# Three moves of order and engine in a four-part encoder trunk: units side by side, a multiply on GpSimd, rows split in two parts

## The chip, the cores and the metric

The kernel runs on one core of a Trainium2 chip. The core has TensorE (matrix products, called PE in the profile; its weight loads are PEld), VectorE (DVE), ScalarE (ACT), GpSimd (POOL) and SyncE (SP, which here issues transfers). The metric is the device time of one execution in microseconds. Before the change three runs took 2383.26, 2383.97 and 2384.84 us; their median is 2383.97 us.

## The reference

An encoder trunk of two layers over 512 positions of width 1024, in float32:

```python
def swiglu(x, w_gu, w_down):
    g, u = jnp.split(x @ w_gu, 2, axis=-1)
    return (jax.nn.silu(g) * u) @ w_down
...
for i in range(DEPTH):
    h = h + 0.5 * swiglu(rmsnorm(h, ffn1_norm[i]), ffn1_w_gu[i], ffn1_w_down[i])
    hn = rmsnorm(h, mix_norm[i])
    # layer 0: ssd_mixer(hn, ...), a state space scan in both directions
    # layer 1: neighbourhood_attention(hn, ...)
    h = h + 0.5 * swiglu(rmsnorm(h, ffn2_norm[i]), ffn2_w_gu[i], ffn2_w_down[i])
    gate = jax.nn.sigmoid(rmsnorm(h, ple_norm[i]) @ ple_w_gate[i])
    h = h + gate * rmsnorm(p[i] @ ple_w_proj[i], ple_post_norm[i])
```

`rmsnorm(x, g)` is x times the reciprocal root of its mean square times a gain g. Inside the SSD mixer the projection of hn has 65 blocks of 128 columns; behind the scan stand another rmsnorm (over 2048 columns) and the output product.

## The kernel before, in words

**Layout.** Activations lie transposed: 128 features on the partitions, 512 positions along the free axis. The residual `h` is eight such tiles. A matrix product in float32 is made of three products in the reduced type fp32r: each operand is cut into a high part and a low part, and `gemm` (L176) issues, for each of eight (or seven) k blocks, high weight times high data (L181), high weight times low data (L184) and low weight times high data (L185). A **unit** is one 128 x 1024 block of weights, so 24 matmuls of 128x512.

**Weights.** `plan` (L121) gives all units in the order of use. `load_unit` (L153) has SP fetch one into `wr` (4 buffers), `split_unit` (L161) makes the high part `wh` on ACT (L166) and the low part `wl` on DVE (L168), with 3 buffers each, and `unit` (L171) keeps three units made ahead of TensorE. So the buffers of a unit are free for the third one behind it when its last matmul has read them.

**Data.** `split(dst, src, gain)` (L187) cuts data in the same way. Without a gain it is a copy on ACT (L189) and a subtraction on DVE (L190); with a gain it is an ACT activation with a scale (L192) and a DVE scalar_tensor_tensor (L193). `Norm.prep` (L256) does this for each residual tile as soon as it is final, with the gain of the next norm, and has the square of the tile summed (L213 on ACT, L217 on GpSimd, or on DVE for the last tile). The norm's factor per position, R, comes later from that sum (`factor`, `rsqrt`, L219: a matmul with ones at L221, then eleven DVE operations, L199 to L205) and is multiplied into the products, not into the data.

**Feed-forward.** `ffn` (L279) runs 22 pairs of units (gate and up) in three chunks, with the chunk's down units behind each. For the first pair the gate unit's eight k blocks run first, then the up unit's eight, then R is made. `activate` (L311) multiplies by R on DVE (L313, L317), takes SiLU on ACT and multiplies the two on GpSimd (L318). There are four feed-forwards; the very first one has an order of its own (`first`). The third follows the gated embedding of layer 0 (`ple`, L377), whose last tile takes a DVE multiply, a tanh on ACT, and two more DVE operations in two halves (L388 to L391), and then `prep`.

**SSD.** `ssd` (L419) begins with unit `ptd` (step sizes) and the first unit of group 0, and makes R between (L435). Units 1 and 2 of group 0 still use the data without R (`norm.pairs`), and their convolution multiplies R in (`conv`, L506, L509). From unit 3 on, the data are `xn`, with R and gain multiplied in: the loop at L450 to L454 makes each of the eight tiles on DVE (L452), then splits it without a gain (L189, L190). `steps` (L456) works out step sizes and decays with many small DVE operations, and writes rows to DRAM (`crow`, `vrow`), from which ACT's L558 reads later. `project` (L523) runs eight units a group; `conv` is one ACT activation (L513), four DVE operations (L517), a tanh (L520) and a DVE product (L521). `scan` (L563) is a generator whose steps run between the next group's units: transposes on TensorE (L577), copied by ACT (L581), multiplied on GpSimd (L585), and so on.

**SSD output.** The output product over 2048 columns is done in two halves of eight row tiles each. The rows 0 to 7 lie in DRAM, are fetched by `early_rows` (L729) at the sixth of group 7's eight units, and are split with the norm's gain by `pairs_of` (L740: L192, L193). Before the change all eight are split at the eighth of these units (i == 7, L773), ahead of the last group's first scan step, whose transposes need ACT too. `out_half` (L751) then runs the first half's units between the last group's scan steps.

**Attention.** `keys` (L817) runs units 0 to 3, then 4 to 7; after unit 0 it makes R. Products lie in five PSUM banks (`mm_bank`); `px_bank` has three more.

**Order.** The program is written in the order of the code, but a planner that builds it sets the order on each engine: it walks through the program with planned durations, and gives an engine that comes free the ready instruction that stands first in the code. At run time each engine follows that order strictly, and waits where an input is late. So a matmul whose input the planner holds to be late can be passed by later ones; one whose input is late only at run time can't.

Of the kernel before, what the change touches and what calls it, by code (L numbers as in the profile page):

```python
# [47 lines left out]
def trunk(ctx, tc, A, out):  # L48
# [55 lines left out]
    def col(i):  # L104
        return cst[:, i:i + 1]
# [70 lines left out]
    def gemm(pt, w, pairs, first=True, last=True, off=0, cols=slice(0, T), behind=False):  # L176
        hi, lo = w
        n = len(pairs)
        for k, xp in enumerate(pairs):
            sl = slice((off + k) * P, (off + k + 1) * P)  # L180
            m = te.matmul(out=pt, lhsT=hi[:, sl], rhs=xp[:, 0, cols], start=first and k == 0, stop=False)  # L181
            if behind and k == 0:
                tc.keep_in_program_order(m)
            te.matmul(out=pt, lhsT=hi[:, sl], rhs=xp[:, 1, cols], start=False, stop=False)  # L184
            te.matmul(out=pt, lhsT=lo[:, sl], rhs=xp[:, 0, cols], start=False, stop=last and k == n - 1)  # L185

    def split(dst, src, gain):  # L187
        if gain is None:
            cast = s.copy(out=dst[:, 0, :], in_=src)  # L189
            v.tensor_sub(out=dst[:, 1, :], in0=src, in1=dst[:, 0, :])  # L190
        else:
            cast = s.activation(out=dst[:, 0, :], in_=src, func=AF.Copy, scale=gain)  # L192
            v.scalar_tensor_tensor(out=dst[:, 1, :], in0=src, scalar=gain, in1=dst[:, 0, :],  # L193
                                   op0=ALU.mult, op1=ALU.subtract)
        return cast
# [83 lines left out]
    def ffn(norm, nxt, between=lambda: None, first=None):  # L279
        R = [None]  # L280
        mids = {}

        held = []

        def gate_up(f):
            pg = mm_bank()
            if not (first and R[0] is None and f == 2):
                pu = mm_bank()
            if first and f < 2:
                held.append((f, pg, pu))  # L290
                if f == 1:
                    first([p for x in held for p in x[1:]], norm.pairs)
                    norm.begin()
                return
            gemm(pg, unit(), norm.pairs)
            if first and R[0] is None:
                pu, w = px_bank(), unit()
                gemm(pu, w, norm.pairs[:4], last=False)
                R[0] = norm.end()
                while held:  # L300
                    activate(*held.pop(0))
                gemm(pu, w, norm.pairs[4:], first=False, off=4)
            else:
                gemm(pu, unit(), norm.pairs)
            if R[0] is None:
                R[0] = norm.factor()
            held.append((f, pg, pu))
            while held:
                activate(*held.pop(0))

        def activate(f, pg, pu):  # L311
            gm = t2()
            v.tensor_mul(out=gm, in0=pg, in1=R[0])  # L313
            sg = sc()
            s.activation(out=sg, in_=gm, func=AF.Silu)
            um = t2()
            v.tensor_mul(out=um, in0=pu, in1=R[0])  # L317
            g.tensor_mul(out=um, in0=um, in1=sg)  # L318
            m = md(F32R)
            split(m, um, None)  # L320
            mids[f] = m

        def down(c, finish=None):
            a, b = CHUNKS[c]
            for d in range(KD):
                pt = mm_bank()
                gemm(pt, unit(), [mids[f] for f in range(a, b)])
                v.scalar_tensor_tensor(out=h[d], in0=pt, scalar=0.5, in1=h[d], op0=ALU.mult, op1=ALU.add)  # L328
                if c == len(CHUNKS) - 1:
                    nxt(d)  # L330
                if d == 2 and finish is not None:
                    finish()

        for c in range(len(CHUNKS)):
            for f in range(*CHUNKS[c]):
                gate_up(f)
            if c:
                down(c - 1)
        made = between()
        if made is None:  # L340
            down(len(CHUNKS) - 1)
            return
        down(len(CHUNKS) - 1, made[1])
        return made[0]
# [74 lines left out]
    def ssd(norm, nxt):  # L419
# [29 lines left out]
        xn = []  # L449
        for k in range(KD):  # L450
            t = t2()
            v.scalar_tensor_tensor(out=t, in0=hk[k], scalar=col(norm.gain + k), in1=R, op0=ALU.mult, op1=ALU.mult)  # L452
            xn.append(md(F32R))
            split(xn[k], t, None)  # L454

        def steps():  # L456

# [307 lines left out]
        for gi in range(NG):  # L765
            beside = project(gi + 1) if gi + 1 < NG else out_half()
            sn = scan(gi, *cur, e0)
            if gi == NG - 1:
                next(sn)
            for i, r in enumerate(beside):  # L770
                cur = r
                if i == 7 and gi == NG - 2:
                    prs = pairs_of(range(8))  # L773
                next(sn, None)
                if i == 5 and gi == NG - 2:
                    early_rows()
                if i == 6 and gi + 1 < NG:
                    e0 = expo(gi + 1, 0)
# [31 lines left out]
    def attention(norm, nxt):  # L810
# [6 lines left out]
        def keys(js):  # L817

            nonlocal R
            kst = px_bank()  # L820
            raw = []
            for j in js:
                pt = mm_bank()
                gemm(pt, unit(), norm.pairs)
                if R is None:
                    R = norm.factor()
                if j % 2 == 0:
                    kt = md()
                kj = kt[:, j % 2, :]
                v.tensor_mul(out=kj, in0=pt, in1=R)  # L830
                q = t2()
                s.activation(out=q, in_=kj, func=AF.Square)
                o = M_SEL + 16 * j + 2 * js[0]
                te.matmul(out=kst[:8], lhsT=msk[:, o:o + 8], rhs=q, start=j == js[0], stop=j == js[-1])
                raw.append(kj)
            m, rk, ra = sc(), sc(), sc()
            v.tensor_scalar(out=m[:8], in0=kst[:8], scalar1=EPS, scalar2=None, op0=ALU.add)
            newton_rsqrt(m[:8], rk[:8], ra[:8])
            rkd = dp.tile([8, T], F32, name=nm("rkd"))
            sy.dma_start(out=rkd, in_=rk[:8])  # L840
            for i in range(4):
                rb = sc()
                for a in range(2):
                    r_ = slice(a * 64, (a + 1) * 64)
                    sy.dma_start(out=rb[r_], in_=rkd[2 * i + a:2 * i + a + 1, :].to_broadcast([64, T]))
                v.scalar_tensor_tensor(out=rb, in0=raw[i], scalar=gqk, in1=rb, op0=ALU.mult, op1=ALU.mult)
                kn = md(F32R)
                split(kn, rb, None)
                kz.append(kn)
# [328 lines left out]
```

## Time and profile before

| | |
|---|---|
| median of three runs | 2383.97 us |
| the profiled execution's own time | 2384.19 us |
| its span on the core | 2382.4 us |
| TensorE busy | 2368.6 us |
| VectorE busy | 1414.6 us |
| ScalarE busy | 957.3 us |
| GpSimd busy | 443.3 us |
| mean granted TensorE clock | 0.999 |

The page of the profile gives busy time by engine, and groups of instructions by line. A row of a group reads: line, engine, operation, out<-in by the program's names, count, then busy time and mean duration, then the idle time of the engine just before these instructions and what ended it. A row of the timeline reads: start, duration (both in us from the span's start), engine, line, operation, count of merged instructions, and in brackets the idle time before and its releaser. Matmuls overlap: one of 128x512 is shown with some 0.39 us, but the next starts some 0.23 us after it, so what is lost on TensorE is read from the distance of two starts. A row of the waits reads: engine and line, whom it waited for, us in total, times, the longest.

### The profile page before, as it was taken

The page shows a single profiled execution, that of the slowest core. Times are in us where ns is not written, and L with a number is a line of the kernel's source. Part 1 is how long each engine was busy: PE and PEld are TensorE (multiplying, and loading weights), DVE is VectorE, ACT ScalarE, POOL GpSimd, SP SyncE. Part 2 cuts the span into 40 slices and gives each one's busy share as a digit, 9 for nine tenths or more (in the row PEclk, how much of TensorE's full clock was granted, in tenths as well). Part 3 has the DMA queues.
Part 4 walks back from the last instruction along what each step waited for, and adds up shares of the span by engine and source line. Part 5 has one row for each costly group of instructions (what it writes and reads, how often), then busy time and mean ns, then how long its engine had stood idle before and what let it go on. Part 6 is the DMA issues. An engine that isn't in the chain of part 4 may idle for free.

```text
span 2382.4 us, 29262 instructions
## 1 busy us (share of the span) xinstructions
PE 2368.6 (99%) x11464; PEld 1953.0 (82%) x11464; DVE 1414.6 (59%) x1893; ACT 957.3 (40%) x1560; POOL 443.3 (19%) x373
## 2 busy tenths in 40 slices
PE   9999999999999999999999999999999999999999
PEld 8888888888888888888888788888877888888887
DVE  6453447877777858554446755444568855544456
ACT  5222324655555653322224433222337753322242
POOL 1110100444555541110103111000100011100120
PEclk9999999999999999999999999999999999999999
DMA  5333233544444452333333233333433332233332
GB/s 180 98 96 99 90 119 104 169 134 142 142 141 139 157 166 89 98 97 97 95 104 102 80 97 97 98 97 93 138 111 136 98 100 92 95 99 97 106 89 80
DMA packets 89707, 265.58 MB, mean 111 GB/s; under 512 B 10960, under 2 KB 11856, under 8 KB 89568
## 3 DMA queue, kind: packets, MB, share of 16 engines
q1 hardware_dynamic: 89280, 263.56, 35.0%
q8 instruction: 90, 1.47, 0.3%
q14 instruction: 49, 0.40, 0.1%
q10 hardware_dynamic: 288, 0.14, 0.0%
HBM read 253.40 MB, written 10.26 MB: 111 GB/s over the span
## 4 chain that ended last, share of the span: by engine, by line
PE 93%; DVE 4%; ACT 2%; issue 1%; DMA 1%; SPq 0%; POOL 0%; DVEq 0%; ACTq 0%; POOLq 0%
PE ps L181 28%; PE ps L184 28%; PE ps L185 28%; PE ps L657 1%; DVE wl L168 1%; PE ps L635 1%; PE ps L678 1%; PE ps L591 1%; PE ps L577 1%; PE ps L958 1%; PE ps L948 0%; DVE md L193 0%; DVE md L190 0%; PE ps L905 0%; PE ps L939 0%
## 5 line engine op out<-in xcount | busy, mean ns | idle before, releaser
L181 PE MATMUL ps<-md,wh 128*128 128x512 f32 (+1 forms) x3152 | 1236.7, 392 | 3.1 <-ACT md L192 3.1
L185 PE MATMUL ps<-md,wl 128*128 128x512 f32 (+1 forms) x3152 | 1228.5, 390 | 0.7 <-DVE wl L168 0.7
L184 PE MATMUL ps<-md,wh 128*128 128x512 f32 (+1 forms) x3152 | 1227.9, 390 | 0.3 <-DVE md L193 0.3
L166 ACT CAST wh<-wr 128x1024 fp32r<-128x1024 f32 (+1 forms) x401 | 414.7, 1034 | 1019.6 <-PE ps L184 638.7
L181 PEld LDWEIGHTS ps<-md,wh 128*128 128x128 f32 x3152 | 592.3, 188 | 128.2 <-issue 4.2
L184 PEld LDWEIGHTS ps<-md,wh 128*128 128x128 f32 x3152 | 592.3, 188 | 125.2 <-issue 4.9
L185 PEld LDWEIGHTS ps<-md,wl 128*128 128x128 f32 x3152 | 592.2, 188 | 124.9 <-DVE wl L168 1.3
L168 DVE TENSOR_TENSOR wl<-wr,wh 128x1024 fp32r<-128x1024 f32 (+1 forms) x401 | 576.8, 1438 | 157.5 <-ACT wh L166 131.8
L318 POOL TENSOR_TENSOR t<-t,sc 128x512 f32<-128x512 f32 x88 | 122.7, 1396 | 1033.0 <-ACT wh L166 635.4
L217 POOL TENSOR_TENSOR sq<-sq,sq 128x512 f32<-128x512 f32 x71 | 104.9, 1478 | 602.6 <-ACT sq L213 600.2
L317 DVE TENSOR_TENSOR t<-ps,rt 128x512 f32<-128x512 f32 x88 | 60.7, 690 | 258.6 <-PE ps L185 258.6
L328 DVE SCALAR_TENSOR_TENSOR hs<-ps,hs 128x512 f32<-128x512 f32 x96 | 66.3, 691 | 233.0 <-PE ps L185 233.0
L313 DVE TENSOR_TENSOR t<-ps,rt 128x512 f32<-128x512 f32 x88 | 60.8, 690 | 127.9 <-PE ps L185 125.6
L517 DVE SCALAR_TENSOR_TENSOR t<-ps,ccw,t 128x510 f32<-128x510 f32 (+1 forms) x180 | 134.0, 745 | 3.1 <-ACT t L513 0.3
L570 POOL TENSOR_TENSOR sc<-sc,sc 128x512 f32<-128x512 f32 x64 | 98.1, 1552 | 66.3 <-ACT sc L560 66.2
L189 ACT CAST md<-t 128x512 fp32r<-128x512 f32 x96 | 59.4, 623 | 121.3 <-POOL t L318 119.3
L558 ACT ACTIVATE sc<-hs,md 128x128 f32<-128x128 f32 x256 | 82.4, 396 | 2.9 <-DMA hs<-crow 2.9
L190 DVE TENSOR_TENSOR md<-t,md 128x512 fp32r<-128x512 f32 x96 | 67.9, 711 | 18.9 <-ACT md L189 18.4
L192 ACT ACTIVATE md<-hs,cst 128x512 fp32r<-128x512 f32 x64 | 46.0, 723 | 50.2 <-DVE hs L798 19.8
L520 ACT ACTIVATE t<-t 128x512 f32<-128x512 f32 x48 | 30.2, 630 | 78.6 <-DVE t L517 78.0
L585 POOL TENSOR_TENSOR md<-md,md 128x256 f32<-128x256 f32 x64 | 45.9, 751 | 84.1 <-ACT md L581 84.1
L193 DVE SCALAR_TENSOR_TENSOR md<-hs,cst,md 128x512 fp32r<-128x512 f32 x64 | 50.6, 794 | 13.7 <-ACT md L192 13.7
(169 smaller groups left out, 1366.7 us busy)
## 6 DMA issues: line engine op xcount, KB each, us to landing
wr<-in_w_gu_dram SPq DMA_DIRECT2D x172, 512.0 KB, 3.5
wr<-in_w_in_dram SPq DMA_DIRECT2D x65, 512.0 KB, 3.6
wr<-in_w_dn_dram SPq DMA_DIRECT2D x64, 448.0 KB, 3.3
wr<-in_w_dn_dram SPq DMA_DIRECT2D x32, 512.0 KB, 3.5
hs<-crow SPq DMA_DIRECT2D x64, 256.0 KB, 3.8
wr<-in_w_qkv_dram SPq DMA_DIRECT2D x24, 512.0 KB, 3.5
hs<-vrow SPq DMA_DIRECT2D x64, 128.0 KB, 4.0
wr<-in_w_out_dram SPq DMA_DIRECT2D x16, 512.0 KB, 4.2
```

The lines of the kernel that those rows point to most:

```text
L166: splits.append(s.copy(out=hi[:, :n], in_=raw[:, :n]))
L168: v.tensor_sub(out=lo[:, :n], in0=raw[:, :n], in1=hi[:, :n])
L181: m = te.matmul(out=pt, lhsT=hi[:, sl], rhs=xp[:, 0, cols], start=first and k == 0, stop=False)
L184: te.matmul(out=pt, lhsT=hi[:, sl], rhs=xp[:, 1, cols], start=False, stop=False)
L185: te.matmul(out=pt, lhsT=lo[:, sl], rhs=xp[:, 0, cols], start=False, stop=last and k == n - 1)
L190: v.tensor_sub(out=dst[:, 1, :], in0=src, in1=dst[:, 0, :])
L217: (v if fast else g).tensor_add(out=self.acc, in0=self.acc, in1=q)
L318: g.tensor_mul(out=um, in0=um, in1=sg)
L328: v.scalar_tensor_tensor(out=h[d], in0=pt, scalar=0.5, in1=h[d], op0=ALU.mult, op1=ALU.add)
L517: v.scalar_tensor_tensor(out=a[:, lo:hi], in0=src[:, lo + o:hi + o], scalar=w(j), in1=a[:, lo:hi], op0=ALU.mult, op1=ALU.add)
L558: s.activation(out=e[:, cs(c)], in_=cb[:, cs(c)], func=AF.Relu, scale=-1.0, bias=cum[:, dr, c, hd:hd + 1])
L570: g.tensor_mul(out=es[j], in0=es[j], in1=cbm[j % 2])
```

## The change

Three edits. A new helper, `side_by_side`, takes two units at once: seven k blocks of the first, seven of the second, then the eighth of each. The feed-forwards other than the first use it for their first pair, and `keys` for its first two units; in `keys` R is made after both. In `ssd` the multiply that makes `xn` is done on GpSimd without the gain, and the gain goes into the split. The row tiles 4 to 7 of the SSD output are split after the first scan step of the last group.

```diff
+    def side_by_side(pts, pairs, behind=False):
+
+        ws = [unit() for _ in pts]
+        k = len(pairs) - 1
+        for pt, w in zip(pts, ws):
+            gemm(pt, w, pairs[:k], last=False, behind=behind)
+            behind = False
+        for pt, w in zip(pts, ws):
+            gemm(pt, w, pairs[k:], first=False, off=k)
...
-            gemm(pg, unit(), norm.pairs)
+            if R[0] is None and not first:
+                side_by_side((pg, pu), norm.pairs)
+            else:
+                gemm(pg, unit(), norm.pairs)
...
-            else:
+            elif R[0] is not None:
                 gemm(pu, unit(), norm.pairs)
...
-            v.scalar_tensor_tensor(out=t, in0=hk[k], scalar=col(norm.gain + k), in1=R, op0=ALU.mult, op1=ALU.mult)
+            g.tensor_mul(out=t, in0=hk[k], in1=R)
             xn.append(md(F32R))
-            split(xn[k], t, None)
+            split(xn[k], t, col(norm.gain + k))
...
             if gi == NG - 1:
                 next(sn)
+                prs += pairs_of(range(4, 8))
...
                 if i == 7 and gi == NG - 2:
-                    prs = pairs_of(range(8))
+                    prs = pairs_of(range(4))
...
-                pt = mm_bank()
-                gemm(pt, unit(), norm.pairs)
-                if R is None:
+                if j == 0:
+                    pts = [mm_bank(), mm_bank()]
+                    side_by_side(pts, norm.pairs)
                     R = norm.factor()
+                if j < 2:
+                    pt = pts[j]
+                else:
+                    pt = mm_bank()
+                    gemm(pt, unit(), norm.pairs)
```

## The prediction

> **What bounds the kernel now.** First the page and its busy times, then who TensorE waits for over the whole span.
>
> ```profile
> span 2382.4 us, 29262 instructions
> ...
> PE 2368.6 (99%) x11464; PEld 1953.0 (82%) x11464; DVE 1414.6 (59%) x1893; ACT 957.3 (40%) x1560; POOL 443.3 (19%) x373
> ```
>
> ```profile
> PE ps L181 <- ACT md L192: 3.4, 2, 3.1
> PE ps L577 <- ACT md L581: 1.3, 1, 1.3
> PE ps L577 <- DVE md L521: 1.1, 1, 1.1
> ...
> PE ps L185 <- DVE wl L168: 0.7, 1, 0.7
> ```
>
> TensorE is the bound: 2368.6 of 2382.4 us. The change takes no matmul away, so it can only win back waits, and there are few: the four rows come to 6.5 us. Four places matter, and each is looked at in the timeline.
>
> *Place 1, the third feed-forward, behind the gated embedding.* TensorE, then VectorE, then ScalarE, then the clock:
>
> ```profile
> 1348.61 0.39 PE L184 MATMUL ps<-md,wh 128*128 128x512 f32 x1
> 1348.84 0.39 PE L185 MATMUL ps<-md,wl 128*128 128x512 f32 x1
> 1352.32 0.73 PE L181 MATMUL ps<-md,wh 128*128 128x512 f32 x2 [3.09 <-ACT md L192]
> 1353.11 0.50 PE L184 MATMUL ps<-md,wh 128*128 128x512 f32 x1
> ```
>
> ```profile
> 1348.62 1.55 DVE L168 TENSOR_TENSOR wl<-wr,wh 128x1024 fp32r<-128x1024 f32 x1
> 1350.10 0.75 DVE L390 SCALAR_TENSOR_TENSOR t<-t,md 128x256 f32<-128x256 f32 x2
> 1350.77 0.75 DVE L391 TENSOR_TENSOR hs<-hs,t 128x256 f32<-128x256 f32 x2
> 1352.30 0.75 DVE L193 SCALAR_TENSOR_TENSOR md<-hs,cst,md 128x512 fp32r<-128x512 f32 x1 [0.79 <-ACT md L192]
> ```
>
> ```profile
> 1351.55 0.72 ACT L192 ACTIVATE md<-hs,cst 128x512 fp32r<-128x512 f32 x1 [2.34 <-DVE hs L391]
> ```
>
> ```profile
> 1353.00:1356.50 3.50, 3.45 (x10) 2.68 (x10) 1.88 (x3) 1.04 (x1) 0.00 (x0) 0.59 0.03 11
> 1356.50:1360.00 3.50, 3.50 (x15) 2.85 (x15) 0.00 (x0) 0.00 (x0) 0.00 (x0) 0.93 0.44 150
> ```
>
> Matmuls start 0.23 us apart (1348.61, 1348.84). At 1349.07 TensorE has done seven of the gate unit's eight k blocks; the eighth tile's high part is ready only at 1352.27, since VectorE made a weight remainder (L168) ahead of the embedding's last operations. Then the granted clock (seventh column of the windows) falls to 0.59 and 0.93. Lost: 1352.32 - 1348.84 - 0.23 = 3.25; two matmuls and a small wait up to 1353.11, 0.79 - 0.46 = 0.33; clock, 0.41 x 3.5 + 0.07 x 3.5 = 1.7. Together some **5.2 us**.
>
> *Place 2, the second feed-forward, behind the SSD:*
>
> ```profile
> 931.34 0.39 PE L181 MATMUL ps<-md,wh 128*128 128x512 f32 x1
> 932.01 0.50 PE L184 MATMUL ps<-md,wh 128*128 128x512 f32 x1 [0.28 <-DVE md L193]
> ```
>
> 0.67 - 0.23, and 0.1 on the slower matmul behind it: **0.55 us**.
>
> *Place 3, the SSD's start.* Windows by engine (PE, PEld, DVE, ACT, POOL), then VectorE's groups from 380 to 392:
>
> ```profile
> 380.00:397.70 17.70, 17.70 (x81) 14.38 (x81) 17.53 (x27) 10.12 (x17) 0.00 (x0) 1.00 0.18 56
> 397.70:416.00 18.30, 17.65 (x78) 14.27 (x77) 17.57 (x30) 6.79 (x9) 1.61 (x2) 1.00 0.28 91
> ```
>
> ```profile
> L452 DVE SCALAR_TENSOR_TENSOR t<-hs,cst,rt 128x512 f32<-128x512 f32 x8 | 5.5, 735 | 0.0
> L190 DVE TENSOR_TENSOR md<-t,md 128x512 fp32r<-128x512 f32 x8 | 5.0, 676 | 0.0
> ```
>
> VectorE has no gap for 36 us (35.1 busy), GpSimd does nothing in the first half. TensorE loses a little at 410:
>
> ```profile
> 409.20 0.39 PE L181 MATMUL ps<-md,wh 128*128 128x512 f32 x1
> 409.43 0.39 PE L184 MATMUL ps<-md,wh 128*128 128x512 f32 x1
> 409.65 0.39 PE L181 MATMUL ps<-md,wh 128*128 128x512 f32 x1
> 409.88 0.39 PE L184 MATMUL ps<-md,wh 128*128 128x512 f32 x1
> 410.92 0.50 PE L185 MATMUL ps<-md,wl 128*128 128x512 f32 x1 [0.65 <-DVE wl L168]
> ```
>
> ```profile
> 409.65 1.22 DVE L168 TENSOR_TENSOR wl<-wr,wh 128x1024 fp32r<-128x1024 f32 x1
> ```
>
> 1.04 - 0.23 = 0.8 us for a weight remainder. The order is telling: two pairs L181, L184 before the first L185, so the planner knew the remainder to be late and passed one L185, but not by enough. Later there is the wait of 1.1 us for L521 (second fence):
>
> ```profile
> 431.99 0.99 ACT L558 ACTIVATE sc<-hs,md 128x128 f32<-128x128 f32 x3 [2.85 <-DMA hs<-crow]
> 432.88 0.61 ACT L520 ACTIVATE t<-t 128x512 f32<-128x512 f32 x1
> ```
>
> ScalarE stood 2.85 us for the decay rows from DRAM with L520, which L521 needs, queued behind.
>
> *Place 4, the SSD output's rows,* on ScalarE:
>
> ```profile
> 822.51 0.58 ACT L539 ACTIVATE t<-ps 128x512 f32<-128x512 f32 x1
> 822.99 1.94 ACT L192 ACTIVATE md<-t,cst 128x512 fp32r<-128x512 f32 x3
> 824.83 1.05 ACT L581 COPY md<-ps 128x512 f32<-128x512 f32 x2
> ```
>
> Three row splits stand ahead of the copies for which TensorE waits 1.3 us.
>
> **The change part by part.**
>
> *Feed-forwards.* Nothing is added to any engine but order. Seven k blocks of the up unit, 21 x 0.23 = 4.8 us, go between 1349.07 and the gate unit's eighth block, so this block starts at 1353.9. Its parts are ready at 1352.27 and 1353.05 (1352.30 + 0.75): 1.6 and 0.8 us of cover. The wait goes, and with it the low clock: **-5.2**. If the cover were gone, TensorE would wait for the excess alone. Next in line would be weights: the gate unit's buffers come free 4.8 us later, at 1354.5; the next cast (some 1.0) and remainder (up to 1.55, L168 above) end by 1357.2, and that unit is wanted at 1353.9 + 6 x 0.23 + 24 x 0.23 = 1360.8. SP's fetch of one weight unit moves up with the second `unit` call; it waits for a raw buffer as before. Place 2: **-0.55**. The fourth feed-forward has no wait of TensorE at its start: 0.
>
> *Keys.* No row of TensorE's waits lies there: 0 to win. R comes one unit (5.5 us) later; first use now:
>
> ```profile
> 1726.47 1.89 DVE L830 TENSOR_TENSOR md<-ps,rt 128x512 f32<-128x512 f32 x3
> ```
>
> From 1726.5 it goes to 1732; three products already wait there, and unit 3 ends only behind that. Five banks cover it; if they ran out, TensorE would wait for the excess. Cost 0.
>
> *Rows.* Two of the three splits of 1.94 us (rows 4 and 5) go behind L581, which then starts 1.3 us earlier: the wait of 1.3 shrinks to some 0.2, **-1.1**. Their place is taken by the first blocks of the output product (rows 0 to 3: 12 x 0.23 = 2.8 us) and the scan's own matmuls, so rows 4 and 5 have time. No transfer moves: the rows' fetches stay where they are. Bounds: -1.3, and +0.5 if row 4 came late.
>
> *Multiply on GpSimd.* Eight L452 leave VectorE (5.5 us), its eight remainders turn from 0.68 into 0.75 (L193 at 1352.30; +0.6), ScalarE's casts cost 0.1 more each. GpSimd gets eight multiplies of two SBUF tensors. The trace has no such multiply here; the nearest group is of the same size, with min/median/max:
>
> ```profile
> L570 POOL TENSOR_TENSOR sc<-sc,sc x64: 1272/1297/2290, 447.1 to 855.6; 128x512 f32<-128x512 f32 x64
> ```
>
> So 1.3 us alone and 2.3 at worst, that is 10.4 to 18.3 us for eight, from 380.2. How they stand to VectorE is seen at 838.6, where a pair of them meets a weight remainder, which takes 1.22 us by itself (409.65):
>
> ```profile
> 838.58 2.40 DVE L168 TENSOR_TENSOR wl<-wr,wh 128x1024 fp32r<-128x1024 f32 x1 [5.04 <-ACT wh L166]
> ```
>
> ```profile
> 838.59 3.54 POOL L570 TENSOR_TENSOR sc<-sc,sc 128x512 f32<-128x512 f32 x2
> ```
>
> VectorE needs 2.40, its own 1.22 and nearly one multiply; the pair needs 3.54, its own 2.6 and nearly one remainder. They take turns and don't overlap. By the Trainium skill (SBUF — State Buffer, section "SBUF: two separate sides") the two engines share a port pair under an exclusive lock, which a VectorE operation with two SBUF inputs contends for against GpSimd, and the loser blocks for the whole instruction. By that rule the multiplies are not free beside the splits; the trace agrees, with 2.40 against 1.22.
>
> Now VectorE step by step. 380.2 to 380.9 L446, then L509 (from PSUM, 0.7). From 382.8 each remainder of `xn` (two SBUF inputs, 0.75) waits for a multiply of 1.3: first remainder 383.5, a weight remainder 386.0, then 388.0, 390.05, 392.1, 394.15, 396.2; GpSimd is through, and the last two end at 396.95 and 397.7. TensorE reads the eighth at some 397.8 (unit 3 starts at 392.8, 0.68 a block): just in time. But VectorE's other work is late. By 397.7 it had done 17.5 - 5.5 - 5.0 = 7.0 us of it; now it has done 0.7 + 0.7 + 1.2 = 2.6. It is **4.4 us behind** in a stretch where it has no gap, so the remainder of 409.65 would come 4.4 us later. The planner can cover that by passing L185s: 16 of a unit's 24 matmuls need no remainder, four ran, so 12 x 0.23 = 2.7 more. Left: **+1.7** (bounds: -1.9, if nothing is lost to turns and both waits, 0.8 and 1.1, go; +4.4, if nothing is passed). I take 1.7, as the rows show both the turns and the passing. The wait for L521 I leave at 1.1: decays and convolution move together.
>
> Sum: -5.2 - 0.55 - 1.1 + 1.7 = -5.15. The profiled execution took 2384.19 us (span 2382.4 and 1.8 around it), 0.2 above the median of 2383.97: 2384.19 - 5.15 = **2379.0 us**.
>
> **The rivals.**
>
> *A: GpSimd frees VectorE.* If the turns are cheaper than at 838.6, the 5.5 us taken off VectorE end both waits: -6.85 - 1.9, **2375.4**. For it: GpSimd idle, VectorE without a gap. Against it: 2.40 for 1.22.
>
> *B: the 4.4 us are not covered.* The planner holds VectorE faster than it is (it passed one L185 where four were wanted), so it might pass too few: -6.85 + 4.4, **2381.7**.
>
> *C: the side-by-side order doesn't meet the wait,* because the second unit's split, now earlier in the code, pushes the embedding's last operations on VectorE back by the time won. Then place 1 stays as it is: -0.55 - 1.1 + 1.7 + about 0.6 for the later weights, **2384.8**. Against it: that split has to wait for the gate unit's buffers, free only at 1354.5.
>
> *D, slower than before: VectorE's lag reaches TensorE twice.* The place is the SSD's start: 4.4 us at the weight remainder and 4.4 again at L577 near 433, as the decay rows come late and ScalarE's order holds L520 behind them. Each idle stretch is then over 3.09 us, after which the clock fell at place 1 (1.7 us each, so 3.4): 12.2 - 6.85 = +5.35, **2389.5**. It decides from 6.85 us lost at the SSD's start. For it: 2.85 us of ScalarE's wait for `crow`. Against it: TensorE's first delay gives the second chain the same time. The Trainium skill (TensorE: Matmul & The Clock Gate, section "What's actually happening") has the clock halve after an idle window of about 3.4 us; here 3.09 us of idling were enough, so D's condition goes by the row.
>
> **How the numbers follow.** Forecast 0.40, A 0.28, B 0.20, C 0.05, D 0.07. A measurement of this kernel tells about 0.2% from no change: 4.8 us, so faster is below 2379.2 and slower above 2388.7. The forecast lies on the edge; half of it counts as faster. Faster: 0.28 + 0.20 = 0.48. Slower: D, 0.07. Same: 0.45. Range: A to B with about 1.5 us for the rows and the small terms above, and the same below cut to 0.6, since A already takes every wait away: **2374.8 to 2383.2**, leaving out C and D. The forecast's own range is 2377 to 2381.
>
> **What would show it.** Place 1: no idle TensorE before the eighth block and a granted clock of 1.00 there; a wait left would speak for C. Place 3: GpSimd's eight multiplies at over 1.3 us mean and VectorE's remainders at over 0.75, L185s passed in the units after unit 3, and a wait of TensorE on `wl`; no such wait speaks for A, one of 3 us and more for B, two for D. Place 4: L581 right behind one L192. Keys: no wait. Wrong altogether would be a planner that puts the work of the SSD's start in another order on VectorE than the step by step above.

## The result, and the profile after

The changed kernel takes 2387.41 us (median of 22 runs, 2386.24 to 2389.18) against 2384.28 us of the kernel before (22 runs on the same chips): ratio 1.0014, 95% interval 1.0008 to 1.0021, so 3.1 us slower. The prediction, 2379.0 us with a range of 2374.8 to 2383.2, is wrong, and in the other direction.

Lines of the changed kernel are shifted: L192, L193 are now L202, L203 (split with gain); L452 is L465, on GpSimd; L477 and L481 (last operation of the decays, and the matmul that reads it) are L490 and L494; L509, L517, L520, L521 (convolution) are L522, L530, L533, L534; L577, L581 are L590, L594; L687, L688 are L700, L701. L166 to L185 keep their numbers.

The page, and whom TensorE waits for:

```profile
span 2387.3 us, 29267 instructions
...
PE 2372.0 (99%) x11464; PEld 1957.0 (82%) x11464; DVE 1411.8 (59%) x1885; ACT 957.9 (40%) x1560; POOL 456.9 (19%) x381
```

```profile
PE ps L184 <- DVE md L203: 2.8, 3, 2.0
PE ps L181 <- ACT wh L166: 1.8, 1, 1.8
PE ps L494 <- DVE md L490: 1.4, 1, 1.4
PE ps L590 <- ACT md L594: 1.3, 1, 1.3
...
PE ps L185 <- DVE wl L168: 1.1, 2, 0.7
```

VectorE is busy only 2.8 us less, although eight operations of 0.7 us left it, and TensorE is busy 3.4 us longer for the same 11464 matmuls, mostly for a lower clock. The old wait of 3.1 us for L192 is gone; four new ones stand in its place (two in the row of L203, one each for L166 and L490), while that for the copies (L594) is as long as before. Compared matmul by matmul (times of the kernel before), the profiled execution falls 5.2 us behind in the SSD's start (by 452 us) and another 6.0 us at the SSD output's rows (by 836 us). It wins back 0.6 us in the second feed-forward (932 us) and 5.3 us in the third (by 1361 us); the span is 4.9 us longer. This execution took 2389.18 us, the longest of the 22, and its mean granted clock of 0.997 is the lowest of them. One at 1.000 took 2386.47 us, so the loss does not hang on a lower clock alone.

**Place 1, the third feed-forward.** TensorE is 10.5 us late here, so the stretch that began at 1349.07 begins at 1359.6. The eighth tile's high part on ScalarE, its first matmul on TensorE, then windows of TensorE, VectorE and so on, with the granted clock in the seventh column:

```profile
1362.11 0.72 ACT L202 ACTIVATE md<-hs,cst 128x512 fp32r<-128x512 f32 x1 [2.35 <-DVE hs L404]
```

```profile
1364.37 0.39 PE L181 MATMUL ps<-md,wh 128*128 128x512 f32 x1
```

```profile
1359.60:1363.00 3.40, 3.40 (x16) 2.82 (x15) 2.61 (x6) 1.05 (x3) 0.05 (x1) 1.00 0.32 83
1363.00:1366.50 3.50, 3.50 (x16) 2.63 (x14) 1.56 (x3) 1.78 (x3) 0.00 (x0) 1.00 0.17 69
```

The high part is ready at 1362.83, 1.5 us before TensorE comes to it. TensorE has no gap, and the clock stays at 1.00 where it was 0.59 before.

**Place 3, the SSD's start.** First the eight multiplies on GpSimd (min/median/max in ns), then VectorE's eight remainders:

```profile
L465 POOL TENSOR_TENSOR t<-hs,rt x8: 1289/1735/1742, 380.3 to 391.3; 128x512 f32<-128x512 f32 x8
```

```profile
L203 DVE SCALAR_TENSOR_TENSOR md<-t,cst,md 128x512 fp32r<-128x512 f32 x8 | 10.5, 1310 | 3.1 <-ACT md L202 3.1
```

A multiply takes 1.29 us alone and 1.74 in turn with a remainder; a remainder 1.31 instead of 0.75. With 3.1 us of waiting between them, VectorE spends 13.6 us on the eight, where the sixteen operations before took 10.5. ScalarE and TensorE at the end of this stretch:

```profile
393.05 0.72 ACT L202 ACTIVATE md<-t,cst 128x512 fp32r<-128x512 f32 x1 [0.97 <-POOL t L465]
393.67 1.98 ACT L166 CAST wh<-wr 128x1024 fp32r<-128x1024 f32 x2
```

```profile
394.75 0.50 PE L181 MATMUL ps<-md,wh 128*128 128x512 f32 x1 [1.83 <-ACT wh L166]
395.09 0.56 PE L184 MATMUL ps<-md,wh 128*128 128x512 f32 x1
396.34 0.79 PE L185 MATMUL ps<-md,wl 128*128 128x512 f32 x1 [0.70 <-DVE wl L168]
396.93 0.63 PE L181 MATMUL ps<-md,wh 128*128 128x512 f32 x1
397.36 0.63 PE L184 MATMUL ps<-md,wh 128*128 128x512 f32 x1
```

The weight casts of units 3 and 4 stand on ScalarE behind all eight L202, six of which wait 0.97 us each for GpSimd. In the kernel before they stood between the copies of the tiles:

```profile
381.51 1.04 ACT L166 CAST wh<-wr 128x1024 fp32r<-128x1024 f32 x1
387.12 1.05 ACT L166 CAST wh<-wr 128x1024 fp32r<-128x1024 f32 x1
```

So TensorE waits 1.83 us for a cast, then 0.70 for the remainder behind it, and from 396.93 two matmuls start 0.43 us apart instead of 0.23: the clock is halved. The third piece comes later, at the matmuls that read the decays, on VectorE and TensorE:

```profile
419.44 0.41 DVE L490 SCALAR_TENSOR_TENSOR md<-md,ea 128x256 f32<-128x256 f32 x1
```

```profile
420.00 1.13 PE L494 MATMUL ps<-md,msk 128*128 128x128 f32 x8 [1.44 <-DVE md L490]
```

VectorE finishes the decays at 419.85, 3.5 us later than L477 in the kernel before (416.39).

**Place 4, the rows.** ScalarE, VectorE, GpSimd, TensorE, and the windows' clock:

```profile
828.78 1.03 ACT L166 CAST wh<-wr 128x1024 fp32r<-128x1024 f32 x1
829.72 1.07 ACT L594 COPY md<-ps 128x512 f32<-128x512 f32 x2
```

```profile
830.41 1.21 DVE L168 TENSOR_TENSOR wl<-wr,wh 128x1024 fp32r<-128x1024 f32 x1
835.22 1.09 DVE L701 TENSOR_TENSOR sc<-sc,md 128x512 f32<-128x512 f32 x1 [3.59 <-POOL sc L700]
...
836.83 1.07 DVE L203 SCALAR_TENSOR_TENSOR md<-t,cst,md 128x512 fp32r<-128x512 f32 x1
```

```profile
833.60 0.61 POOL L598 TENSOR_TENSOR md<-md,md 128x256 f32<-128x256 f32 x1
834.17 1.01 POOL L700 TENSOR_TENSOR sc<-sc,hs 128x384 f32<-128x384 f32 x1
```

```profile
837.95 0.50 PE L184 MATMUL ps<-md,wh 128*128 128x512 f32 x1 [1.95 <-DVE md L203]
```

```profile
838.89:845.70 6.81, 6.19 (x16) 4.80 (x16) 1.83 (x2) 6.01 (x16) 6.81 (x9) 0.50 0.51 148
```

The copies that TensorE waits for hardly started earlier: they come 1.97 us after the first of the transposes, 2.20 us before the change, since a weight cast (L166) took the place on ScalarE that the splits left. And row 4's remainder, moved back, now stands on VectorE behind L701 (the gate's product of an output tile of the scan), which waits 3.59 us for GpSimd's L700 (the sum of that tile), itself queued among GpSimd's multiplies L598. Row 5's split waits on ScalarE as well, behind the square of that tile. TensorE waits 1.95 and 0.62 us, and runs 6.8 us at half clock from 838.89 on. In the kernel before, VectorE stood at the same spot, with no row behind it:

```profile
831.25 1.08 DVE L688 TENSOR_TENSOR sc<-sc,md 128x512 f32<-128x512 f32 x1 [3.15 <-POOL sc L687]
```

### The profile page after: what moved, and what is told of

It is laid out like the page before. It is cut to its first block, busy times and chain, and to the rows that moved or that the text cites. A ratio compares the mean times of both kernels' runs of the same rounds, so it can differ in the third digit from the quotient of the medians.

```text
span 2387.3 us, 29267 instructions
## 1 busy us (share of the span) xinstructions
PE 2372.0 (99%) x11464; PEld 1957.0 (82%) x11464; DVE 1411.8 (59%) x1885; ACT 957.9 (40%) x1560; POOL 456.9 (19%) x381
## 4 chain that ended last, share of the span: by engine, by line
PE 94%; DVE 2%; POOL 1%; issue 1%; ACT 1%; DMA 0%; SPq 0%; POOLq 0%; ACTq 0%; DVEq 0%
PE ps L181 29%; PE ps L185 29%; PE ps L184 29%; PE ps L670 1%; PE ps L691 1%; PE ps L648 1%; PE ps L977 1%; PE ps L604 1%; POOL t L465 1%; PE ps L590 1%; PE ps L967 0%; DVE t L530 0%; POOL sc L583 0%; PE ps L924 0%; PE ps L958 0%
## 5 line engine op out<-in xcount | busy, mean ns | idle before, releaser
L185 PE MATMUL ps<-md,wl 128*128 128x512 f32 (+1 forms) x3152 | 1230.2, 390 | 1.1 <-DVE wl L168 1.1
L166 ACT CAST wh<-wr 128x1024 fp32r<-128x1024 f32 (+1 forms) x401 | 414.0, 1034 | 1006.8 <-PE ps L184 612.4
L185 PEld LDWEIGHTS ps<-md,wl 128*128 128x128 f32 x3152 | 593.1, 188 | 125.6 <-DVE wl L168 2.4
L530 DVE SCALAR_TENSOR_TENSOR t<-ps,ccw,t 128x510 f32<-128x510 f32 (+1 forms) x180 | 134.0, 744 | 3.7 <-ACT t L526 0.9
L200 DVE TENSOR_TENSOR md<-t,md 128x512 fp32r<-128x512 f32 x88 | 62.9, 715 | 18.9 <-ACT md L199 18.3
L533 ACT ACTIVATE t<-t 128x512 f32<-128x512 f32 x48 | 30.3, 631 | 97.5 <-DVE t L530 97.0
L202 ACT ACTIVATE md<-hs,cst 128x512 fp32r<-128x512 f32 x64 | 46.0, 723 | 50.7 <-DVE hs L812 19.8
L598 POOL TENSOR_TENSOR md<-md,md 128x256 f32<-128x256 f32 x64 | 45.1, 736 | 77.0 <-ACT md L594 77.0
L203 DVE SCALAR_TENSOR_TENSOR md<-hs,cst,md 128x512 fp32r<-128x512 f32 x64 | 51.6, 811 | 13.9 <-ACT md L202 13.9
```

The lines of the kernel that those rows point to most:

```text
L166: splits.append(s.copy(out=hi[:, :n], in_=raw[:, :n]))
L530: v.scalar_tensor_tensor(out=a[:, lo:hi], in0=src[:, lo + o:hi + o], scalar=w(j), in1=a[:, lo:hi], op0=ALU.mult, op1=ALU.add)
```

## The experiments

Each was timed against the kernel before on the same chip; differences are of medians.

**1 to 3: each part alone.** The side-by-side edit of `ffn` and `keys`:

```diff
+            if R[0] is None and not first:
+                side_by_side((pg, pu), norm.pairs)
...
+                if j == 0:
+                    pts = [mm_bank(), mm_bank()]
+                    side_by_side(pts, norm.pairs)
```

> The kernel before with the side-by-side units alone (feed-forwards and keys). Theory: this part did what the prediction's sum gave it (5.2 us at the third feed-forward with the low clock behind it, 0.55 at the second), and the loss lies in the two other edits: 5 to 6.5 us faster than before, no TensorE wait at 1349 and no half clock there. Rival: the third feed-forward's wait went only because TensorE was already some 10 us late by then (the residual's last tile keeps its own pace behind the embedding, so this can hardly be): then the gain is under 3 us here.

2378.19 against 2384.07 us, ratio 0.9974 (0.9964 to 0.9984): -5.9. This part does what was worked out for it, and alone it beats both kernels. The multiply alone:

```diff
-            v.scalar_tensor_tensor(out=t, in0=hk[k], scalar=col(norm.gain + k), in1=R, op0=ALU.mult, op1=ALU.mult)
+            g.tensor_mul(out=t, in0=hk[k], in1=R)
-            split(xn[k], t, None)
+            split(xn[k], t, col(norm.gain + k))
```

> The kernel before with the multiply on GpSimd alone. Theory: in the changed kernel TensorE was 5.2 us later than before at 452 us, so this edit alone costs 4.5 to 6 us: about 1.8 us of wait for the weight cast L166, 1.0 for its remainder, 2 for the half clock behind them, 2 in smaller waits, with the waits of before (0.8 and 1.1) partly gone. Rival (the prediction's step): 1.7 us for VectorE's lag alone, if the rest comes from the interplay with the other edits.

2389.52 us, ratio 1.0022 (1.0013 to 1.0031): +5.45, with the same three losses as in the changed kernel (1.8 for the cast, 1.0 for remainders, 1.4 for the decays, and 6.8 us of half clock). The rows alone:

```diff
+                prs += pairs_of(range(4, 8))
-                    prs = pairs_of(range(8))
+                    prs = pairs_of(range(4))
```

> The kernel before with the rows split in two parts alone. Theory: in the changed kernel TensorE lost 5 us more between 823 and 860 than before, through the remainders of rows 4 and 5, which stand on VectorE behind an operation that waits for GpSimd, and through a half clock; so this edit alone costs 4 to 6 us. Rival: the planner lays these instructions otherwise when the first two edits are not there; then between 1.1 us faster and 1 us slower.

2388.49 us, ratio 1.0019 (1.0010 to 1.0028): +4.4, where -1.1 was forecast. The parts add up to -5.9 + 5.45 + 4.4 = +3.95; together they came to +3.1. So they hardly touch each other, and there are two causes to find.

**4: weights cut ahead.** With the multiply on GpSimd, one more weight unit, unit 3, is cut into parts ahead of the multiplies in the code (two units are cut already), so that its cast does not stand behind all of them on ScalarE:

```diff
+        while len(ready) < 3:
+            split_unit()
         xn = []
```

> The multiply on GpSimd alone, with the next weight unit's split ahead of the eight tiles in the code, so that its cast on ScalarE (L166) stands behind the first of the eight and its remainder on VectorE behind the first of its eight. Theory Q (ScalarE's queue is the cause: the cast waits behind eight activations that wait for GpSimd one by one): the wait of 1.8 us, the 1.0 behind it and the half clock go, and the kernel is within 1.5 us of before. Theory L (turns of GpSimd and VectorE are the cause): VectorE is still some 4 us behind afterwards, the waits come back at a later weight remainder, and 3 us or more of the loss stay.

2391.05 us, ratio 1.0029 (1.0017 to 1.0040): +7.0. The waits for cast and remainder did go, but TensorE's waits now begin with:

```profile
PE ps L483 <- DVE md L479: 6.9, 1, 6.9
```

L479 here is the decays' last operation; it ends at 421.34, 4.95 us later than before. So ScalarE's queue decided where VectorE's lag was paid. As the cause by itself it fell.

**5 and 6: the multiply taken away, and added.** First the tiles are split from the residual with the gain alone, so the factor R is missing and no engine multiplies:

```diff
-            t = t2()
-            v.scalar_tensor_tensor(out=t, in0=hk[k], scalar=col(norm.gain + k), in1=R, op0=ALU.mult, op1=ALU.mult)
-            split(xn[k], t, None)
+            split(xn[k], hk[k], col(norm.gain + k))
```

> The kernel before, with the multiply that makes the SSD's normalised tiles left out: the eight tiles are split straight from the residual with the gain, and the factor R is missing in them. So VectorE is rid of the 5.5 us and GpSimd gets nothing. Theory (the turns of VectorE and GpSimd eat the gain): without turns the freed 5.5 us end the waits of 0.8 and 1.1 us at 410 and 433, so 1 to 3 us faster than before. Rival (the splits' new form and order on ScalarE and VectorE are to blame, with or without GpSimd): slower than before by 2 us or more.

2382.83 against 2384.50 us, ratio 0.9991 (0.9982 to 1.0000): -1.7; the decays end at 410.90, 5.5 us earlier than before. So taking the multiply off every engine is worth 1.7 us here (the interval reaches from 4.3 to 0), and the new form of the splits is not what made the kernel slower. Second, the kernel before with eight more multiplies on GpSimd whose results nobody reads:

```diff
+            g.tensor_mul(out=sc(), in0=hk[k], in1=R)
```

> The kernel before, with the eight GpSimd multiplies added and their results read by nobody; VectorE makes the tiles as before. Theory (turns): VectorE waits for up to eight multiplies of 1.3 us while it does the same work as before, so its remainders and the decays come 6 to 10 us later and the kernel is 3 us or more slower; GpSimd's multiplies and VectorE's operations with two SBUF inputs are longer by one another. Rival (the loss comes from instructions that wait for GpSimd's results): nobody waits, so within 1 us of before.

2393.70 us, ratio 1.0037 (1.0023 to 1.0051): +9.2. Nothing waits for these multiplies; VectorE's groups and TensorE's first wait read:

```profile
L190 DVE TENSOR_TENSOR md<-t,md 128x512 fp32r<-128x512 f32 x8 | 9.4, 1226 | 0.0
L453 DVE SCALAR_TENSOR_TENSOR t<-hs,cst,rt 128x512 f32<-128x512 f32 x8 | 9.2, 1197 | 0.0
```

```profile
PE ps L185 <- DVE wl L168: 7.3, 1, 7.3
```

L453 is L452 of the kernel before. The same sixteen operations took 5.0 + 5.5 us before; here 18.6, so 8.1 us more without any idling: the turns alone. The decays end 8.6 us late (425.02).

**7: half of the multiplies on GpSimd.**

```diff
+            if k % 2:
+                g.tensor_mul(out=t, in0=hk[k], in1=R)
+                split(xn[k], t, col(norm.gain + k))
+            else:
+                v.scalar_tensor_tensor(out=t, in0=hk[k], scalar=col(norm.gain + k), in1=R, op0=ALU.mult, op1=ALU.mult)
+                split(xn[k], t, None)
```

> The kernel before, with four of the eight multiplies (every other one) on GpSimd. Theory (turns): four multiplies take 5.2 us of turns and save VectorE 2.7, so it is some 2 us late, about half of the loss of all eight: 1 to 4 us slower than before. Rival: with only every other tile on GpSimd the two engines work beside each other and VectorE wins 2.7 us: 0.5 to 2 us faster.

2391.06 us, ratio 1.0026 (1.0016 to 1.0036): +6.6, more than with all eight. This was a miss. VectorE loses less to turns and has the decays done at 414.99, 1.4 us *earlier* than before, and yet TensorE waits for a cast and a remainder:

```profile
PE ps L181 <- ACT wh L166: 3.6, 1, 3.6
PE ps L185 <- DVE wl L168: 3.5, 1, 3.5
```

```profile
406.12 0.63 ACT L524 ACTIVATE t<-t 128x512 f32<-128x512 f32 x1 [4.88 <-DVE t L521]
...
407.72 1.03 ACT L166 CAST wh<-wr 128x1024 fp32r<-128x1024 f32 x1
```

ScalarE stands 4.88 us for a convolution on VectorE (L521 here is L517 of the kernel before) with the cast queued behind. VectorE's work is less than before, but its order is another: the remainder of the weight unit wanted next runs at 411.84, not at 401.30. Sixteen operations have come ahead of it, six of the decays and ten of the convolutions; as four multiplies have left, it stands twelve places further back. (The expectation of run 11 below counts eleven places and four operations.)

**10 to 12: is it the order?** First the next weight unit cut ahead, as in 4, with half of the multiplies on GpSimd:

> The kernel before with every second multiply of the SSD's start on GpSimd, as in the earlier run that came out 6.6 us slower, and with the three next weight units cut into parts ahead of the eight multiplies in the code. In the earlier run the decays were done 1.4 us earlier than before, but TensorE waited 3.8 us for a weight cast and 3.7 us for a weight remainder between 404 and 413 us; ScalarE stood 4.9 us waiting for a convolution on VectorE with that cast queued behind. Theory (the order of ScalarE's and VectorE's queues made those waits, not the amount of work on VectorE): with the weight units cut earlier the order changes, both waits shrink under 1 us each and the loss falls to at most 2 us against the kernel before. Rival (VectorE has no slack here, and whatever is put first makes something else late): one wait goes and another of 3 us or more takes its place, and the loss stays at 4 us or more.

2391.06 against 2383.87 us, ratio 1.0030 (1.0018 to 1.0042): +7.2. The edit left VectorE's order in this stretch as it was, and the two waits are still there (3.6 and 3.1 us), so it tells nothing about the order. Then, with half of the multiplies on GpSimd, `steps` one unit further back in the code:

```diff
-            if i == 2:
+            if i == 3:
                 steps()
```

> Every second multiply of the SSD's start on GpSimd, as in the earlier run (6.6 us slower than before, with waits of 3.8 us for a weight cast and 3.7 us for a weight remainder between 404 and 413 us), and the step sizes and decays (steps) moved one unit further back in the code. Cutting the next weight units ahead of the multiplies had changed nothing: VectorE's order stayed as it was, with the remainder of one weight unit eleven places further back than in the kernel before, behind four steps of the decays and the convolution between them. Moving steps back puts that remainder ahead of the decays again. Theory (the place of that one remainder in VectorE's order made the two waits): both waits shrink under 1 us and no half clock follows, the loss is at most 1.5 us, and with VectorE 1.4 us ahead the time may come out up to 1 us under the kernel before. Rival (VectorE has no slack in any order): a wait of 3 us or more for the decays or a weight remainder appears in 405 to 425, and the loss stays at 4 us or more.

2387.65 against 2384.09 us, ratio 1.0013 (1.0004 to 1.0022): +3.6. The wait for the cast is gone; a half clock of 3.4 us stays, and the row for remainders is:

```profile
PE ps L185 <- DVE wl L168: 3.0, 1, 3.0
```

Between the two theories: 3 us of the 6.6 belong to the place of that one remainder, and the next remainder then stands behind decays and convolution in the same way. And the control, `steps` moved in the kernel before:

> The kernel before with step sizes and decays moved one unit further back in the code, nothing else: the control for the run with half of the multiplies on GpSimd and the same move. VectorE's work is that of the kernel before; the decays end later by about one unit's convolution, some 4 us, and the matmuls that read them are one unit later as well. Theory (only places in the order change): within 1 us of the kernel before; the wait of 0.7 us for a weight remainder at 410 may go. Rival (the decays are the end of a chain that TensorE waits for at once): 2 us or more slower, with a wait at the matmuls behind the decays.

2383.57 us, ratio 0.9998 (0.9989 to 1.0006): no change. So the move itself is worth nothing. Why the planner sets the remainder back in 7 is not settled.

**8: the rows without GpSimd in front of VectorE.** The rows' edit, and the sum that VectorE's L688 waits for is made on VectorE itself for that group's second tile:

```diff
-                    g.tensor_add(out=y[:, rg], in0=y[:, rg], in1=vb[:, rg])
+                    (v if gi == NG - 2 and j else g).tensor_add(out=y[:, rg], in0=y[:, rg], in1=vb[:, rg])
```

> The rows split in two parts, and the two additions (L687) of the last but one group's second tile moved from GpSimd to VectorE, so that VectorE's L688, which stands ahead of the remainders of rows 4 and 5, no longer waits for GpSimd. Theory (these remainders were late only because VectorE's queue stood at L688): the waits of 2.1 and 0.6 us and the half clock at 830 go, and of the 4.4 us of the rows' loss 3 us or more; the wait for the copies L581 (1.3) stays. Rival (rows 4 and 5 are late by themselves, behind the copies on ScalarE): 3 us or more of the loss stay.

2385.28 against 2384.50 us, ratio 1.0003 (0.9994 to 1.0012): +0.8. TensorE's waits from 820 to 860 us:

```profile
PE ps L577 <- ACT md L581: 0.8, 1, 0.8
PE ps L184 <- DVE md L193: 0.3, 1, 0.3
```

The two waits for row remainders have shrunk to one of 0.3 us and the half clock is gone: 3.6 of the 4.4 us, so the sum queued on GpSimd, behind which VectorE's queue stood, was most of the rows' loss. The gain of 1.1 does not come either: the wait for L581 goes from 1.3 to 0.8, and matmul by matmul 0.9 us are lost again at the remainders of rows 4 and 5.

**9: the last scan one step later,** on top of the side-by-side edit:

```diff
-            if gi == NG - 1:
-                next(sn)
```

> The side-by-side edit alone, and besides it the last group's scan starts inside the loop of the first half's output units and not one step ahead of it. The side-by-side edit alone was 5.9 us faster than the kernel before, with a wait of about 1.3 us left at the transposes whose copies stand behind the row splits. Theory (that wait is paid only because the transposes stand in front of the output product): the output unit's blocks now come first and cover it, so 1.0 to 1.4 us less than the side-by-side edit alone, about 7 us under the kernel before. Rival (the last scan is a chain as long as the output units beside it, so that a later start comes out at its end): the wait at the transposes goes, another of 1 us or more appears before the end of the SSD output, and the time is that of the side-by-side edit alone or longer, 4 to 6 us under the kernel before.

2382.30 against 2383.87 us, ratio 0.9992 (0.9983 to 1.0001): 4.3 us of the 5.9 lost again. The wait at the transposes did not go, it grew, since their copies now stand behind a square that waits for VectorE, a cast and another copy:

```profile
832.35 0.66 PE L590 MATMUL ps<-msk,md 128*128 128x128 f32 x4 [2.41 <-ACT md L594]
```

```profile
829.76 0.63 ACT L223 ACTIVATE sq<-sc 128x512 f32<-128x512 f32 x1 [4.62 <-DVE sc L701]
830.30 1.03 ACT L166 CAST wh<-wr 128x1024 fp32r<-128x1024 f32 x1
831.23 0.58 ACT L770 COPY md<-ps 128x512 f32<-128x512 f32 x1
831.71 2.05 ACT L594 COPY md<-ps 128x512 f32<-128x512 f32 x4
```

Behind it the clock is halved for 3.4 us; matmul by matmul 3.4 us are lost here and 1.1 more around two small waits near 884 and 891. Theory and rival both had the wait at the transposes gone, and in this both fell. The rival's other half, that a later start is paid at the end of the scan, came in part (the 1.1 us), but with 1.6 us under the kernel before the time lies outside what it gave. The best version measured stays the side-by-side edit alone.

## Why the prediction was wrong, point by point

**Feed-forwards and keys: right.** Forecast -5.75, measured -5.9 for this edit alone and -5.9 in the changed kernel's profile (0.6 + 5.3). The forecast gave the eighth block's high part 1.6 us of cover; it had 1.5. Rival C is excluded.

**Multiply on GpSimd: that turns cost time was right, the order and the cover failed.** The prediction has VectorE "4.4 us behind"; the decays end 3.9 us later with the multiply alone, 3.5 in the changed kernel. That the size comes near is in part luck: a multiply and a remainder together took 1.70 us where the prediction adds them up to 2.05, and it has nothing for the 3.1 us that VectorE idles for ScalarE. By the Trainium skill (SBUF — State Buffer, section "SBUF: two separate sides") a VectorE operation with two SBUF inputs and a GpSimd operation that reads SBUF exclude each other for a whole instruction. Experiment 6 agrees in direction: 18.6 us for 10.5; the 1.70 for 2.04 (1.29 + 0.75) says that a part of the two still overlaps in the profile's times.

The first step that failed is the order in "VectorE step by step". It has a weight remainder at 386.0, behind the first remainder of `xn`. It ran at 395.07, behind all eight, because its cast on ScalarE stood behind all eight activations (393.67; 381.51 before). The prediction's own sign for "wrong altogether", another order on VectorE at the SSD's start, came true.

The second is "The planner can cover that by passing L185s: 16 of a unit's 24 matmuls need no remainder, four ran, so 12 x 0.23 = 2.7 more". A unit's matmuls keep their k order in both kernels; what passes is the first block of the *next* unit. The order before, as the planner wrote it (place, line, operation, tiles), at that spot:

```
1759 L181 MATMUL ps_3015<-md_2693,wh_2938 128x512
...
1761 L181 MATMUL ps_3049<-md_2693,wh_2978 128x512
...
1763 L185 MATMUL ps_3015<-md_2693,wl_2940 128x512
...
1788 L481 MATMUL ps_2858<-md_2684,msk 128x128 x4
```

and after:

```
1759 L181 MATMUL ps_3015<-md_2693,wh_2938 128x512
...
1771 L494 MATMUL ps_2858<-md_2684,msk 128x128 x4
```

After the change no L185 is passed, and the matmul that reads the decays stands 17 places *earlier* (17 x 0.23 = 3.9 us), behind 1764 weight matmuls instead of 1781, while the decays come 3.5 us later. The planner places it as if VectorE had become faster: without any multiply (experiment 5) it stands behind 1757. That the planner doesn't count the turns is shown by experiment 6: with eight multiplies that nobody reads, this matmul keeps its place, behind 1781 weight matmuls in both traces, and VectorE runs 8.6 us late. Here the prediction had the sign of the cover wrong. What the earlier place alone costs, no run separates.

Two losses were in no term of the sum: the wait for ScalarE's casts behind eight activations that wait for GpSimd (1.83 us), and the half clock (0.20 us on each of twelve matmuls, 2.4 us). Start to start, 1.9 at the cast, 1.4 at the remainder, 2.4 of clock, 0.5 and 1.6 at 416 and 420, less the two waits of before (0.8 and, start to start, 1.25) make 5.75; twelve matmuls of the scan (L648) that start closer together than before win 0.8 of it back, which leaves 5.0 where 5.2 were measured. Rival A is excluded. B was right that the planner passes too few, and its +4.4 lies near the +5.45 of the multiply alone, but it has the whole loss at one remainder, where the waits for remainders are 1.0 us. D had the sign, but its second place, the convolution near 433, shows no such wait; the decays at 419 do, and the low clock came after less idling than D asked for. Its 2389.5 us lies near the measurement by luck, as the rows lost what D put at the SSD's start.

**Rows: wrong.** "L581, which then starts 1.3 us earlier" failed: the freed place went to a weight cast. "Rows 4 and 5 have time" failed as well, with its bound of +0.5: VectorE had an operation waiting for GpSimd ahead of them, and ScalarE a square that waits for VectorE. The prediction shows ScalarE's splits at that spot and not VectorE's queue, where the wait of 3.15 us stood already before the change. Start to start, the two waits cost 2.1 and 0.8 us and the half clock 2.9: nearly all of the 6.0 us lost here.

**Sum.** Forecast -5.75 - 1.1 + 1.7; measured alone -5.9 + 4.4 + 5.45. The whole error lies in the two steps that put work behind a wait in an in-order queue.

## What to carry to other kernels

An engine that is full is not relieved by moving two-input work to an engine that it takes turns with: eight operations of 0.7 us taken off VectorE made it 3.5 to 5 us later here, and even taking them away altogether gave 1.7 us. When work is moved back or to another engine, read, on *each* queue it then stands in, what is ahead of it and what that waits for; and remember that a planner which doesn't know the cost places the readers as if the move had succeeded. Side-by-side order, which adds nothing and only fills a known wait with work that is ready, was the one part whose whole forecast came true.

## What the runs showed of the hardware that was not expected

The half clock needs much less than 3 us of idling in one piece. Consecutive windows of the changed kernel (PE busy is the first number behind the comma, the granted clock the seventh column):

```profile
391.75:395.16 3.41, 1.58 (x10) 0.94 (x8) 2.93 (x5) 2.44 (x4) 1.26 (x1) 1.00 0.00 0
395.16:398.57 3.41, 2.71 (x7) 1.82 (x6) 3.30 (x4) 2.14 (x3) 0.00 (x0) 0.50 0.35 83
398.57:401.99 3.42, 3.42 (x9) 2.63 (x8) 3.19 (x6) 1.37 (x3) 0.00 (x0) 0.50 0.68 224
```

1.83 us of idling within one stretch of 3.41 us were followed by two such stretches at 0.50. The drop at 838.89 lies 130 x 3.413 us behind the one at 395.16, and between the two the clock was full for 436.91 us, 128 x 3.413: the stretches run on a fixed grid. By the Trainium skill (TensorE: Matmul & The Clock Gate, section "What's actually happening") the window is 3413 ns, free-running, and the clock halves after an idle window: the grid agrees; that the whole window must be idle does not, as 1.58 us of it were busy.

Laid on this grid, the fourteen traces of this case sort themselves, from 10 us after the start to the last matmul. Of the 9678 stretches at full clock, every one with 1.66 us of idling or more (21) was followed by half clock, and none with 1.48 us or less. A wait of 1.43 us (side-by-side edit alone), which lies whole in the stretch from 432.63 to 436.05, left the clock at 1.00:

```profile
434.56 1.20 PE L590 MATMUL ps<-msk,md 128*128 128x128 f32 x9 [1.43 <-DVE md L534]
```

At half clock less is enough: after 0.41 us of idling or more (10 stretches) it stayed halved, after 0.34 us or less (21) it came back. By this the 0.70 us of waiting for the remainder kept the second stretch slow. These bounds are what the traces show; why they lie there, no run tells. The kernel before shows the first of this too: of its wait of 3.09 us, 2.18 lay in the stretch ahead of the drop at 1353.6.

So in this execution of the changed kernel the two times of half clock cost 2.7 and 2.9 us besides the waits that set them off. The mean granted clock of the 22 executions goes from 0.997 to 1.000, as it would if the grid lay elsewhere to the waits in each of them; only this one has a trace, so that is not shown.
